# A two-layer diffusion backbone step: three temporaries for the pair products, a feed-forward in three parts, another pace for w_ada

## The chip, the cores and the metric

The kernel runs on one core of a Trainium2 chip. The metric is the device time of one execution in microseconds, as the median of several runs. The engines are TensorE (PE in the profile, its weight loads PEld), VectorE (DVE), ScalarE (ACT), GpSimd (POOL) and SyncE (SP), each with its own instruction queue that it works off in order. All DMAs go through the queues of SP and POOL but for three small ones at the start.

## The reference, cut to what matters

Each of two layers applies a token-mixing sub-layer and a SwiGLU feed-forward, both between normalisations, with scales, shifts and gates that come from a conditioning vector through `w_ada`. There are 128 context and 512 latent tokens, so 640 rows of 1024 features, all in float32.

```python
for l in range(DEPTH):                                   # 2
    mod = jax.nn.silu(c) @ w_ada[l] + b_ada[l]           # 6 vectors of 1024
    sh1, sc1, g1, sh2, sc2, g2 = jnp.split(mod, 6, axis=-1)
    h = rms_norm(x, g_pre[0]) * (1 + sc1) + sh1
    # ... combined projection, windowed attention, neighbourhood attention, Fourier mixing, merge
    x = x + g1 * rms_norm(y, g_post[0])
    h = rms_norm(x, g_pre[1]) * (1 + sc2) + sh2
    g, u = jnp.split(h @ w_ffn_in, 2, axis=-1)           # each 640 x 2816
    x = x + g2 * rms_norm((jax.nn.silu(g) * u) @ w_ffn_out, g_post[1])
```

The change lies in the feed-forward: `h @ w_ffn_in` is 640 x 1024 by 1024 x 5632, and `w_ffn_out` takes 2816 features back to 1024.

## The kernel before

**Precision.** TensorE takes each float32 operand as a high and a low part (`whi` and `wlo` for weights, made by ScalarE at L172 and VectorE at L173; `hT_hi` and `hT_lo` for activations), and every product is three matmuls.

**The feed-forward (`ffn`, L1510).** The 2816 features are 22 tiles of 128 columns. `FFN_PARTS` cuts them into parts. For the tiles of one part the kernel first makes gate ("fg") and up ("fu") projections, evacuates them to `aT` as a high and a low part (`evac`, L1530 to L1544), and then multiplies `aT` by the part's rows of `w_ffn_out` and adds the result to `y` (`xstat`, L1402, with `acc_y`, L1577; ScalarE copies in the first part, VectorE adds in the others). A unit of `w_ffn_out` is 256 rows by 512 columns and serves two tiles of a part, for one half of the output and all five token tiles: 30 matmuls of 512 columns. The last part runs through `xstat_tiles` (L1419) instead: the first half of the output runs unit by unit, the second half token tile by token tile, so that each tile's norm (`tail`, L1466) can start while later tiles are still being multiplied. The steps of a tail (residual, square, scale, transposes, split) are put off by the fixed delays in `DELAYS`, and the first projection of the next layer (`mix_open`, L901) needs the first three tiles' results.

**Pairs.** Apart from the first `FFN_SINGLE` = 2 tiles, gate and up projections are made for two column tiles at a time with seven products instead of eight (`pair`, L731): token halves, row halves and the two tiles make a 2 x 2 by 2 x 2 block product. Each product is 12 matmuls of 320 columns. Sums of activations ("S") are made on chip by `sums` (L676); sums of weights (`wsum`) are made in HBM by DMAs (`sum_jobs`, L399), copies on SP's queue (L412) and accumulating additions on POOL's queue (L415), 16 jobs for each part and each of gate and up. Between products the results pass through four temporaries (`m1`, `u2`, `m5`, `u3`) of 128 x 320, and two sets of four alternate; ScalarE writes at L750 and L758, VectorE at L754, L764, L768 and L773, POOL at L765. The temporaries lie in the buffer `mt3`.

**The order of the work.** Everything is written out by a planner with its own clock (`step`, L319): each group of matmuls adds its length at 2.4 columns per ns, and whatever has come due is emitted after it: deferred tasks, sum jobs (every `SUM_DT` microseconds of that clock, 2.9 for layer 0 from 20.0 on, 5.5 for layer 1 from the start of layer 0's feed-forward), and steps of the `w_ada` generator (every `ADA_DT` = 5.0 during pairs and output units). What is left of the sum jobs is flushed at the start of `ffn`; what is left of the `w_ada` steps is flushed by `ada_finish` (L552) before the last part's output units.

**The w_ada side work (`ada_round`, L465).** During the feed-forward the product with `w_ada` runs on VectorE (L498 and L500): eight loads of 512 KB a round on SP's queue, two operations of 128 x 1024 for each, then three steps of lag (`ADA_LAG`), then 16 small matmuls that add over the partitions (L512). Layer 0's feed-forward holds four rounds and layer 1's one. Three buffers of the side tile hold loads ahead.

**Weights.** `wraw` has four buffers of 512 KB; `whi` and `wlo` have three buffers, each of which holds one full unit or two half units of a pair. Two further buffers (`alt_slot`, L129) serve fixed units at the changes of stage, among them the last unit of the first output half and the first unit of the second half of the last part.

Of the kernel before, what the change touches and what calls it, by code (L numbers as in the profile page):

```python
# [10 lines left out]
F32 = mybir.dt.float32  # L11
F32R = mybir.dt.float32r
AF = mybir.ActivationFunctionType
OP = mybir.AluOpType
# [3 lines left out]
T = 640  # L18
# [14 lines left out]
FFN_SINGLE = 2  # L33
ADA_MIX = ([(0, 2), (0, 3), (0, 4)], [(1, 3), (1, 4)])
ADA_FFN = ([(0, 5), (1, 0), (1, 1), (1, 2)], [(1, 5)])
FFN_PARTS = (4, 6, 6, 6)
SUMS_AT = (0.1, 0.2, 2.0, 3.0, 4.0, 5.0, 9.0, 99.0)
SUM_START, SUM_DT, SUM_ROWS = 20.0, (2.9, 5.5), 256
TICK = 2.5
ADA_DT, ADA_LAG = 5.0, 3  # L40
T_TOK, T_KO, T_V = 2.7, 0.9, 2.9
ADA_D0 = 2.1
T_COL, T_OUT, T_GM = 8.0, 5.2, 2.0
# [50 lines left out]
class Weights:  # L94
# [34 lines left out]
    def alt_slot(key):  # L129
# [3 lines left out]
        if kind in ("wo", "fo"):  # L133
            k0 = 0 if kind == "wo" else DFF // 128 - FFN_PARTS[-1]
            k1 = 6 if kind == "wo" else DFF // 128 - 2
# [152 lines left out]
class Kernel:  # L288
# [85 lines left out]
    def pair_ranges():  # L374


        n0 = 0
        for p, nt in enumerate(FFN_PARTS):
            first = n0 if p else FFN_SINGLE
# [351 lines left out]
    def pair(self, key, evac):  # L731

        nc, W = self.nc, self.W
        m1, u2, m5, u3 = (self.tmp[:, 4 * self.tmp_set + i, :] for i in range(4))
        self.tmp_set ^= 1

        def product(i, ps, first, last):
            w, x = W.part(key, i), self.left[i]()
            for k in range(4):
                for j, (p, q) in enumerate(((0, 0), (0, 1), (1, 0))):  # L740
                    nc.tensor.matmul(ps, w[p][:, k, :], x[q][:, k, :], start=first and k == 0 and j == 0,  # L741
                                     stop=last and k == 3 and j == 2, skip_group_check=True)

        def end(i):
            W.part_done(key, i)
            self.step(12 * 320 * PE_COL)
        psum = lambda: self.psum("mm")[:, :320]
        p1 = psum()
        product(0, p1, True, False)
        nc.scalar.activation(m1, p1, AF.Copy)  # L750
        end(0)
        p2 = psum()
        product(1, p2, True, False)
        nc.vector.tensor_tensor(u2, p2, m1, op=OP.add)  # L754
        end(1)
        p3 = psum()
        product(2, p3, True, False)
        nc.scalar.activation(m5, p3, AF.Copy)  # L758
        end(2)
        product(3, p1, False, True)  # L760
        evac(0, p1, 0)
        end(3)
        product(4, p2, False, True)
        nc.vector.tensor_tensor(u3, p2, m1, op=OP.add)  # L764
        nc.gpsimd.tensor_tensor(m5, m5, u3, op=OP.subtract)  # L765
        end(4)
        product(5, p3, False, True)
        nc.vector.tensor_tensor(u2, p3, u2, op=OP.subtract)  # L768
        evac(1, u2, 0)
        end(5)  # L770
        p4 = psum()
        product(6, p4, True, True)
        nc.vector.tensor_tensor(m1, p4, u3, op=OP.add)  # L773
        evac(0, m1, 1)
        evac(1, m5, 1)
        end(6)
# [733 lines left out]
    def ffn(self, l):  # L1510
        nc = self.nc
# [3 lines left out]
        if l + 1 < L:  # L1515
            self.sums_due, self.sums_at, self.sums_dt = deque(self.sum_jobs(l + 1)), self.vt, SUM_DT[1]
        for p, nt in enumerate(FFN_PARTS):
            last = p == len(FFN_PARTS) - 1
            aT = [self.fp.tile([128, 4, T], F32R, name=f"aT{i}", tag=f"mt{i}", bufs=1) for i in range(3)]
            both = aT[2].rearrange("p (a b) t -> p a b t", a=2)  # L1520

            def split_of(j, aT=aT, both=both):

                return (aT[0][:, j, :], aT[1][:, j, :]) if j < 4 else (both[:, 0, j - 4, :], both[:, 1, j - 4, :])

            def lhs(j, t, split_of=split_of):
                return tuple(self.cut(w, t) for w in split_of(j))
            gate = {}

            def evac(kind, n, gate=gate, split_of=split_of, n0=n0):  # L1530
                def f(src, g):
                    c0, c1 = HALVES[g]
                    if n not in gate:
                        gate[n] = self.fp.tile([128, T], F32, name="sg", tag="sg", bufs=2)
                    t = gate[n][:, c0:c1]
                    if kind == "fg":
                        nc.scalar.activation(t, src, AF.Tanh, scale=0.5)
                        nc.vector.scalar_tensor_tensor(t, t, 1.0, src, op0=OP.add, op1=OP.mult)
                        return
                    nc.vector.tensor_tensor(t, t, src, op=OP.mult)  # L1540
                    hi, lo = (w[:, c0:c1] for w in split_of(n - n0))
                    nc.scalar.activation(hi, t, AF.Copy, scale=0.5)
                    nc.vector.scalar_tensor_tensor(lo, t, 0.5, hi.bitcast(F32), op0=OP.mult, op1=OP.subtract)
                return f  # L1544

            first = n0
            if p == 0:
                first = FFN_SINGLE
                seq = [(kind, n) for n in range(first) for kind in ("fg", "fu")]
                self.tmp = self.fp.tile([128, 8, 320], F32, name="tmp", tag="mt3", bufs=1)  # L1550
                self.tmp_set = 0
                for g in range(2):
                    self.run_tasks(GTOK[g])
                    if g:
                        self.sums(self.z, SUMS_AT)
                    for kind, n in seq[:3]:
                        self.proj((l, kind, n), g, evac(kind, n), 4, HALVES)
                self.W.alt.clear()
                for kind, n in seq[3:]:
                    self.proj2((l, kind, n), evac(kind, n), HALVES)  # L1560
                self.run_tasks(("sums",))
                rounds = ADA_FFN[l]
                self.run_tasks(range(5))
                side = self.fp.tile([128, 5, D], F32, name="ada_side", tag="x", bufs=1)
                self.W.side_open([side[:, i, :] for i in range(2, 5)], 8 * len(rounds))
                self.ada = self.ada_rounds(rounds, side[:, 0:2, :])
                self.ada_acc, self.ada_dt = 0.0, ADA_DT
# [170 lines left out]
```

## Time and profile before

| | us |
|---|---|
| median of three runs (2206.36 to 2209.75) | 2206.68 |
| the profiled execution, its own time | 2209.04 |
| span of the profile, first to last instruction | 2207.3 |
| PE busy | 2109.3 |
| VectorE busy | 1287.2 |
| ScalarE busy | 911.7 |
| GpSimd busy | 541.7 |

In the profile, a row of the waits reads: who waited, for whom, total microseconds, times, longest. A row of the timeline reads: start, length, engine, line, operation, output and inputs, shapes, count, and in brackets the engine's idle time before it with what ended it. A row of a stretch reads: its bounds and length, then busy time and number of instructions for PE, PEld, VectorE, ScalarE and POOL, and last the granted clock of TensorE, the busy share of the DMA engines and GB/s. A row of a group reads: line, engine, operation, names, shapes, count, then busy time, mean ns of one, and idle time before them.

### The profile page before, as it was taken

How to read it: one execution, taken by the hardware profiler on the slowest of the kernel's cores; microseconds unless marked ns; L12 is line 12 of the kernel's file. 1: busy time of each engine (PE TensorE's matmuls, PEld its weight loads, DVE VectorE, ACT ScalarE, POOL GpSimd, SP SyncE). 2: the span in 40 equal slices, each digit the busy share in tenths (PEclk: the TensorE clock that was granted, in tenths of full speed). 3: DMA queues.
4: the chain of work that ended last, by engine and by line, in shares of the span. 5: the costliest groups of instructions: out<-in, count | busy, mean ns of one | idle time of the engine just before them, and what ended most of it. 6: DMA issues, size and time to landing. Idle time of an engine off the chain costs nothing.

```text
span 2207.3 us, 36184 instructions
## 1 busy us (share of the span) xinstructions
PE 2109.3 (96%) x13876; PEld 1945.7 (88%) x13876; DVE 1287.2 (58%) x2397; ACT 911.7 (41%) x1944; POOL 541.7 (25%) x815
## 2 busy tenths in 40 slices
PE   6999999999889999999679999999999999999998
PEld 4999989998778998989659999999988799989896
DVE  3555555553238686778754656555533586747475
ACT  3644543432235442434235544444323444424252
POOL 3122245443234111111132111343411320101002
PEclk9999999999999999999889999999999999999999
DMA  7433467777994765888665343556545445434353
GB/s 269 127 81 76 117 163 176 171 180 210 280 236 130 205 188 165 227 226 219 202 182 158 94 92 91 140 130 137 140 137 175 147 148 153 135 105 148 92 153 134
DMA packets 387213, 349.70 MB, mean 158 GB/s; under 512 B 17632, under 2 KB 344320, under 8 KB 386784
## 3 DMA queue, kind: packets, MB, share of 16 engines
q1 hardware_dynamic: 345744, 293.51, 42.2%
q0 software_dynamic: 40864, 53.64, 15.4%
q8 instruction: 109, 1.79, 0.3%
q14 instruction: 64, 0.52, 0.1%
q10 hardware_dynamic: 432, 0.25, 0.0%
HBM read 335.50 MB, written 95.72 MB: 195 GB/s over the span
## 4 chain that ended last, share of the span: by engine, by line
PE 61%; DVE 4%; ACT 2%; issue 1%; POOL 1%; DVEq 0%; POOLq 0%; ACTq 0%
PE ps_mm L741 20%; PE ps_mm L647 7%; PE ps_mm L648 7%; PE ps_mm L649 7%; PE ps_mm L1397 5%; PE ps_mm L1398 5%; PE ps_mm L1399 5%; PE ps_o L849 1%; PE ps_t L836 1%; DVE ada_side L500 1%; PE ps_s L809 1%; PE ps_s L810 1%; DVE wlo L173 1%; DVE x L1474 1%; POOL hT_lo L628 0%
## 5 line engine op out<-in xcount | busy, mean ns | idle before, releaser
L173 DVE TENSOR_TENSOR wlo<-wraw,whi 128x512 fp32r<-128x512 f32 (+1 forms) x453 | 405.9, 902 | 366.3 <-ACT whi L172 360.7
L647 PE MATMUL ps_mm<-hT_hi,whi 128*128 128x256 f32 (+2 forms) x1552 | 490.4, 316 | 7.3 <-ACT whi L172 5.8
L649 PE MATMUL ps_mm<-hT_hi,wlo 128*128 128x256 f32 (+2 forms) x1552 | 482.9, 311 | 4.0 <-DVE wlo L173 4.0
L172 ACT ACTIVATE whi<-wraw 128x512 fp32r<-128x512 f32 (+1 forms) x453 | 354.6, 790 | 310.9 <-PE ps_mm L1399 118.8
L648 PE MATMUL ps_mm<-hT_lo,whi 128*128 128x256 f32 (+2 forms) x1552 | 481.7, 310 | 0.0
L647 PEld LDWEIGHTS ps_mm<-hT_hi,whi 128*128 128x128 f32 x1552 | 293.6, 189 | 17.2 <-ACT whi L172 7.9
L649 PEld LDWEIGHTS ps_mm<-hT_hi,wlo 128*128 128x128 f32 x1552 | 293.1, 189 | 6.3 <-DVE wlo L173 6.3
L648 PEld LDWEIGHTS ps_mm<-hT_lo,whi 128*128 128x128 f32 x1552 | 293.2, 189 | 0.4
L741 PE MATMUL ps_mm<-S,whi 128*128 128x320 f32 x960 | 213.2, 310 | 2.8 <-DVE tmp L754 2.8
L741 PE MATMUL ps_mm<-hT_hi,whi 128*128 128x320 f32 x640 | 198.0, 309 | 4.8 <-ACT tmp L750 4.8
L741 PE MATMUL ps_mm<-hT_hi,wlo 128*128 128x320 f32 x640 | 197.3, 308 | 0.0
L741 PE MATMUL ps_mm<-hT_lo,whi 128*128 128x320 f32 x640 | 197.3, 308 | 0.0
L765 POOL TENSOR_TENSOR tmp<-tmp 128x320 f32<-128x320 f32 x40 | 54.4, 1360 | 567.2 <-DVE tmp L764 508.4
L741 PEld LDWEIGHTS ps_mm<-S,whi 128*128 128x128 f32 x960 | 159.9, 188 | 5.6 <-DVE tmp L754 4.3
L415 POOL DMA_DIRECT2D wsum<-in_w_ffn_in x128 | 119.6, 1022 | 181.3 <-DMA wsum<-wsum 149.8
L1397 PE MATMUL ps_mm<-whi,aT 128*128 128x512 f32 x400 | 159.3, 398 | 0.0
L1398 PE MATMUL ps_mm<-wlo,aT 128*128 128x512 f32 x400 | 158.9, 397 | 0.0
L1399 PE MATMUL ps_mm<-whi,aT 128*128 128x512 f32 x400 | 158.7, 397 | 0.0
L741 PE MATMUL ps_mm<-S,wlo 128*128 128x320 f32 x480 | 148.1, 309 | 0.0
L741 PEld LDWEIGHTS ps_mm<-hT_hi,whi 128*128 128x128 f32 x640 | 120.1, 188 | 7.0 <-ACT tmp L750 6.4
L647 PE MATMUL ps_mm<-o,whi 128*128 128x256 f32 (+1 forms) x384 | 121.6, 317 | 0.0
L741 PEld LDWEIGHTS ps_mm<-hT_lo,whi 128*128 128x128 f32 x640 | 120.1, 188 | 0.3
(236 smaller groups left out, 3978.7 us busy)
## 6 DMA issues: line engine op xcount, KB each, us to landing
wraw<-in_w_in SPq DMA_DIRECT2D x92, 512.0 KB, 4.1
wraw<-wsum SPq DMA_DIRECT2D x160, 256.0 KB, 3.4
wsum<-in_w_ffn_in POOLq DMA_DIRECT2D x96, 384.0 KB, 6.5
wraw<-in_w_ffn_in SPq DMA_DIRECT2D x120, 256.0 KB, 3.3
wraw<-in_w_ada SPq DMA_DIRECT2D x56, 512.0 KB, 4.8
wraw<-in_w_ffn_out SPq DMA_DIRECT2D x44, 512.0 KB, 4.7
ada_side<-in_w_ada SPq DMA_DIRECT2D x40, 512.0 KB, 5.5
wsum<-in_w_ffn_in SPq DMA_DIRECT2D x48, 384.0 KB, 4.7
```

What stands on the lines that cost most here:

```text
L172: self.k.nc.scalar.activation(hi, src, AF.Copy)
L173: self.k.nc.vector.tensor_tensor(lo, src, hi.bitcast(F32), op=OP.subtract)
L415: return lambda: nc.gpsimd.dma_start(out[r], src[r], accum_op=OP.add)
L500: nc.vector.scalar_tensor_tensor(acc[:, s, :], u.raw, c, acc[:, s, :], op0=OP.mult, op1=OP.add)
L647: nc.tensor.matmul(ps, wh, xh[:, c0:c1], start=(k == 0), stop=False)
L648: nc.tensor.matmul(ps, wh, xl[:, c0:c1], start=False, stop=False)
L649: nc.tensor.matmul(ps, wl, xh[:, c0:c1], start=False, stop=(k == K - 1))
L741: nc.tensor.matmul(ps, w[p][:, k, :], x[q][:, k, :], start=first and k == 0 and j == 0, stop=last and k == 3 and j == 2, skip_group_check= ...
L765: nc.gpsimd.tensor_tensor(m5, m5, u3, op=OP.subtract)
L1397: nc.tensor.matmul(ps, xh, u.hi[:, i, :], start=st and i == 0, stop=False)
L1398: nc.tensor.matmul(ps, xh, u.lo[:, i, :], start=False, stop=False)
L1399: nc.tensor.matmul(ps, xl, u.hi[:, i, :], start=False, stop=sp and i == 1)
```

## The change

The parts become 6, 8 and 8 tiles. With two single tiles in the first part, the pairs per part and projection become 2, 4 and 4 (before: 1, 3, 3 and 3). `aT` takes four buffers instead of three, `mt0` to `mt3`: the high parts of tiles 0 to 3 and 4 to 7 in the first two, the low parts in the others. The temporaries leave `mt3` for three tiles of their own; `u3` is written over `m1`, and from one pair to the next `m1` and `u2` swap places, while `m5` keeps its tile. Sum jobs become 96 a layer, of 256 KB in the first part and 512 KB in the others (before: 128 jobs, 128 KB and 384 KB), and are emitted every 3.6 (layer 0) or 7.5 (layer 1). The `w_ada` steps are emitted every 4.2.

```diff
-FFN_PARTS = (4, 6, 6, 6)
+FFN_PARTS = (6, 8, 8)
 SUMS_AT = (0.1, 0.2, 2.0, 3.0, 4.0, 5.0, 9.0, 99.0)
-SUM_START, SUM_DT, SUM_ROWS = 20.0, (2.9, 5.5), 256
+SUM_START, SUM_DT, SUM_ROWS = 20.0, (3.6, 7.5), 256
 TICK = 2.5
-ADA_DT, ADA_LAG = 5.0, 3
+ADA_DT, ADA_LAG = 4.2, 3
...
     def pair(self, key, evac):
-        m1, u2, m5, u3 = (self.tmp[:, 4 * self.tmp_set + i, :] for i in range(4))
-        self.tmp_set ^= 1
+        self.tmp = self.tmp[1], self.tmp[0], self.tmp[2]
+        m1, u2, m5 = self.tmp
...
         product(4, p2, False, True)
-        nc.vector.tensor_tensor(u3, p2, m1, op=OP.add)
-        nc.gpsimd.tensor_tensor(m5, m5, u3, op=OP.subtract)
+        nc.vector.tensor_tensor(m1, p2, m1, op=OP.add)
+        nc.gpsimd.tensor_tensor(m5, m5, m1, op=OP.subtract)
...
         product(6, p4, True, True)
-        nc.vector.tensor_tensor(m1, p4, u3, op=OP.add)
+        nc.vector.tensor_tensor(m1, p4, m1, op=OP.add)
...
         for p, nt in enumerate(FFN_PARTS):
-            aT = [self.fp.tile([128, 4, T], F32R, name=f"aT{i}", tag=f"mt{i}", bufs=1) for i in range(3)]
-            both = aT[2].rearrange("p (a b) t -> p a b t", a=2)
-            def split_of(j, aT=aT, both=both):
-                return (aT[0][:, j, :], aT[1][:, j, :]) if j < 4 else (both[:, 0, j - 4, :], both[:, 1, j - 4, :])
+            aT = [self.fp.tile([128, 4, T], F32R, name=f"aT{i}", tag=f"mt{i}", bufs=1) for i in range(4)]
+            def split_of(j, aT=aT):
+                return tuple(aT[i + j // 4][:, j % 4, :] for i in (0, 2))
...
-                self.tmp = self.fp.tile([128, 8, 320], F32, name="tmp", tag="mt3", bufs=1)
-                self.tmp_set = 0
+                self.tmp = [self.fp.tile([128, 320], F32, name=f"tmp{i}") for i in range(3)]
```

## The prediction

> **What bounds the kernel now.** I read the page first, then TensorE's waits, then the timeline at each long wait, and last the sums over stretches.
>
> ```profile
> span 2207.3 us, 36184 instructions
> PE 2109.3 (96%) x13876; PEld 1945.7 (88%) x13876; DVE 1287.2 (58%) x2397; ACT 911.7 (41%) x1944; POOL 541.7 (25%) x815
> ...
> PE ps_t L512 <- DVE ada_side L500: 15.2, 1, 15.2
> PE ps_mm L647 <- ACT hT_hi L627: 14.6, 3, 10.8
> ...
> PE ps_t L599 <- DVE nt L587: 7.7, 4, 5.8
> PE ps_mm L647 <- ACT whi L172: 5.8, 6, 1.9
> PE ps_s L809 <- DVE sm L811: 5.5, 3, 3.2
> PE ps_t L599 <- ACT y L608: 5.2, 1, 5.2
> ```
>
> TensorE is busy 96% of the span, and the change alters none of its matmuls: both cuts of the 22 feed-forward tiles make 20 pairs a layer and 22 output units. The time can move only through the 98 us in which PE is idle, and through the slow stretch behind each long idle. Those waits sit at a few places, and the change touches most of them.
>
> **A. The w_ada step (ADA_DT 5.0 to 4.2).** The step loop counts planner time: a pair is 7 x 1.6 = 11.2, an output unit 30 x 512/2400 = 6.4. One round takes 19 calls: 16 VectorE operations, two empty calls, and the matmuls of L512 in the 19th; layer 0 has four rounds, 76 calls, the last VectorE operation in call 73. Now, up to `ada_finish`, there are 20 pairs and 4 + 6 + 6 units, 224 + 102.4 = 326.4, so 326.4/5.0 gives 65 calls. Call 65 falls at the very end, and 8 operations are left over: 9 in a row.
>
> ```profile
> 1083.74 10.85 DVE L500 SCALAR_TENSOR_TENSOR ada_side<-ada_side,ada_st 128x1024 f32<-128x1024 f32 x9
> ...
> 1093.54 2.19 PE L512 MATMUL ps_t<-ada_side,ones 128*32 128x256 f32 x16 [15.15 <-DVE ada_side L500]
> 1095.66 0.80 PE L1397 MATMUL ps_mm<-whi,aT 128*128 128x512 f32 x1
> ...
> 1099.64 0.39 PE L1397 MATMUL ps_mm<-whi,aT 128*128 128x512 f32 x1
> 1099.88 0.39 PE L1398 MATMUL ps_mm<-wlo,aT 128*128 128x512 f32 x1
> ...
> 816.52 1.07 PE L512 MATMUL ps_t<-ada_side,ones 128*32 128x256 f32 x16
> ```
>
> After, 20 pairs and 6 + 8 units come to 224 + 89.6 = 313.6, and 313.6/4.2 gives 74 calls. The last VectorE operation is due at 73 x 4.2 = 306.6, four products ahead of the pairs' end; calls 75 and 76, an empty one and the matmuls, are left. VectorE would have to run four products (some 7 us) late for PE to wait. The removed time is 15.15 us, plus what PE loses behind it: 16 matmuls in 2.19 us where an undisturbed round takes 1.07, and nine matmuls from 1095.66 to 1099.64, 3.98 us, where nine at the usual 0.23 (the rows at 1099.64 and 1099.88) take 2.1. Together 15.15 + 1.1 + 1.9 = 18.1 us.
>
> The Trainium skill ("TensorE: Matmul & The Clock Gate", Part 1) says that an idle window of about 3.4 us halves the array's clock, and that about 3.4 us of work restores it. Here the matmuls are 0.44 us apart instead of 0.23, and the slow stretch lasts from 1093.54 to 1099.64, 6 us, so the trace agrees in kind, for longer. By the page the restart would cost 1.7 us and the term 16.9.
>
> **B. The end of layer 0's feed-forward (last part 8 tiles instead of 6).** There each token tile of the second half gets 4 units instead of 3, 24 matmuls instead of 18, while its norm chain on VectorE stays.
>
> ```profile
> 605.85:672.72 66.87, 60.69 (x268) 48.85 (x266) 30.18 (x43) 25.84 (x53) 22.58 (x32) 0.95 0.82 222
> 1095.66:1160.38 64.72, 48.67 (x208) 39.24 (x205) 34.65 (x47) 22.49 (x49) 21.58 (x29) 0.87 0.63 183
> 1700.26:1759.54 59.28, 58.63 (x267) 47.61 (x265) 30.42 (x41) 25.94 (x53) 15.13 (x24) 1.00 0.48 160
> ...
> L1474 DVE SCALAR_TENSOR_TENSOR x<-y,ss,x 128x1024 f32<-128x1024 f32 x5 | 7.4, 1488 | 1.9 <-POOL ss L567 1.9
> L1595 DVE TENSOR_TENSOR y<-y,ps_mm 128x512 f32<-128x512 f32 x10 | 6.7, 683 | 10.9 <-PE ps_mm L1399 10.9
> L606 DVE TENSOR_SCALAR y<-ps_t,a,sh 128x128 f32<-128x128 f32 x12 | 4.1, 399 | 0.0
> L587 DVE TENSOR_SCALAR y<-x,ss 128x1024 f32<-128x1024 f32 x4 | 4.0, 1011 | 5.7 <-POOL ss L567 5.7
> ...
> L1599 DVE TENSOR_TENSOR y<-y,gm 128x512 f32<-128x512 f32 x5 | 3.5, 693 | 4.2 <-ACT junk L635 4.2
> L628 DVE TENSOR_TENSOR hT_lo<-y,hT_hi 128x512 fp32r<-128x512 f32 x3 | 2.1, 689 | 1.2 <-ACT hT_hi L627 1.1
> ```
>
> The first three rows are the output stretches of mix 0, feed-forward 0 and mix 1 (busy time of PE, PEld, DVE, ACT and POOL); mix 1 runs 4 units a tile in 59.28 us with nearly no idle. The others are VectorE's groups near the second stretch. Per tile it owes 7.4/5 + 6.7/5 + 4.1/3 + 4.0/4 + 3.5/5 + 2.1/3 = 6.6 us, and PE gives it 18 x 0.23 = 4.2 us; with 24 matmuls 5.6. The middle stretch holds 180 matmuls (41.9 us) and 24 transposes (about 3.1), so 19.7 us too many, 1.9 already in A: 17.8, 16.05 of it the waits of 5.2 and 10.85. The widened cover saves at least 4 x 1.4 = 5.6 us. At most it becomes like mix 1, 15 us. The deferred steps are due at fixed planner times, so tile 2's transposes, due 9.2 after its end, now come before the last two units (at 20.5 of 23.0, counted from tile 0's end), not after all of them (due 16.9, and the matmuls end at 17.9). One split of the next projection's weights moves later for want of a free buffer: 1.3 us less in the middle of the chain, and hidden by the first projection. I take 11. The output matmuls themselves, the last tile and the kernel's own end stay.
>
> **C. The half-sums (96 jobs a layer instead of 128, larger, further apart).** Bytes are the same: 32 jobs x 128 KB and 96 x 384 before, 32 x 256 and 64 x 512 after. Copies go through SP's queue among the weight loads, additions through POOL's. In layer 0 the last is due at 20 + 127 x 2.9 = 388 now and 20 + 95 x 3.6 = 362 after.
>
> ```profile
> 610.05 3.58 POOL L415 DMA_DIRECT2D wsum<-in_w_ffn_in  x4
> 639.79 0.88 POOL L415 DMA_DIRECT2D wsum<-in_w_ffn_in  x1 [26.16 <-DMA wsum<-wsum]
> ...
> 652.60 0.69 PE L599 MATMUL ps_t<-ident,nt 128*128 128x128 f32 x2 [5.83 <-DVE nt L587]
> ...
> 652.70 0.98 POOL L415 DMA_DIRECT2D wsum<-in_w_ffn_in  x1 [0.94 <-DMA wsum<-wsum]
> ```
>
> Additions due by 364 start at 610.05, so the last one after would start near 620, before POOL's norm steps are wanted (90 + 18 matmuls of 0.233 us after 605.85, about 631). Now POOL stands 26.16 us before a late copy with those steps queued behind; PE waits 5.83. Mix 0's stretch is 66.87 against mix 1's 59.28: 7.6 is the most to gain, 0 the least, if the 512 KB transfers land as late. I take 5.5. Elsewhere in mix 0 the denser sums (512/3.6 against 384/2.9 KB, +7%) press on SP's weight loads and on POOL's bias loads; the whole-run waits for whi (5.8) and for L811 (5.5) are their present price. I charge 2, from -4 to +6. In layer 1 the last job moves from 698.5 to 712.5 after the feed-forward's start, still some 50 ahead of the output projection: nothing.
>
> **D. VectorE in the pair stretches.**
>
> ```profile
> 761.34:838.72 77.38, 75.58 (x521) 74.27 (x520) 64.62 (x106) 36.92 (x74) 14.85 (x17) 1.00 0.69 192
> 880.54:958.78 78.24, 76.39 (x523) 74.55 (x522) 65.03 (x109) 36.32 (x73) 14.91 (x17) 1.00 0.83 229
> 1000.61:1078.39 77.78, 75.97 (x523) 74.39 (x521) 64.35 (x109) 36.21 (x73) 16.23 (x19) 1.00 0.87 230
> 2082.44:2156.29 73.85, 73.85 (x506) 73.84 (x504) 53.34 (x95) 36.33 (x73) 8.21 (x6) 1.00 0.48 143
> ...
> L500 DVE SCALAR_TENSOR_TENSOR ada_side<-ada_side,ada_st 128x1024 f32<-128x1024 f32 x70 | 91.0, 1315 | 0.0
> ...
> SPq L153 <- DVE ada_side L500: 22.0, 21, 5.7
> ```
>
> Six pairs take 73.85 us without w_ada work and 3.5, 4.4 and 3.9 more with it; 1.07 each is L512, so 8.6 us is PE held up by VectorE. Up to the last operation, pairs now hold 224/5.0 x 16/19 = 37.7 operations, after (224 - 7)/4.2 x 16/19 = 43.5: 5.8 more at 91.0/70 = 1.3 us, 7.5 us, less whatever slack takes. Three long stretches also recover one time less than four, about 2.5. From 0 to 10, I take 6. Each pair of calls also issues 512 KB on SP, behind which weight loads queue while it waits for L500 (last row); four raw buffers cover that. Twenty fewer additions at L1582 (0.69 us) save VectorE work only in stretches where PE has no wait: nothing.
>
> **E. Three temporaries.** They add waits: POOL's m5 - m1 before L773 overwrites m1, and L750 and L758 (ScalarE) behind the evacuations of the pair before.
>
> ```profile
> 2129.39 1.20 POOL L765 TENSOR_TENSOR tmp<-tmp 128x320 f32<-128x320 f32 x1 [11.39 <-DVE tmp L764]
> ...
> 2132.80 0.48 DVE L773 TENSOR_TENSOR tmp<-ps_mm,tmp 128x320 f32<-128x320 f32 x1
> ...
> 2134.76 0.49 DVE L1540 TENSOR_TENSOR sg<-sg,tmp 128x320 f32<-128x320 f32 x1
> ...
> 2137.55 0.43 ACT L758 ACTIVATE tmp<-ps_mm 128x320 f32<-128x320 f32 x1
> ```
>
> POOL is done 2.2 us before L773; m5's last reader 2.3 us before L758. If that cover went, ScalarE's splits and with them PE's weights would queue behind VectorE. Cost 0, and the fourth mt buffer and the new split of tiles cost nothing either: their readers are earlier matmuls on the same in-order PE.
>
> **Sum.** -18.1 - 11 - 5.5 + 2 + 6 = -26.6. The profiled execution took 2209.04 us around its span; that gives 2182.4. It lay 2.4 above the median, 2206.68, from which I predict 2180.
>
> **The rivals.**
> 1. The tail does not shrink beyond the work bound and POOL stays blocked: B 5.6, C 0, so -18.1 - 5.6 + 2 + 6 = -15.7, 2191. For it: the due times are fixed numbers, and VectorE still owes 6.6 us to 5.6. Against: mix 1's stretch.
> 2. The larger transfers hold SP and POOL in mix 0: C 0 and +8 there: 2206.7 - 18.1 - 11 + 8 + 6 = 2192. For: DMA share 0.82 at mix 0's end. Against: the same bytes.
> 3. Slower: the temporaries bind. With VectorE later by more than the 2.3 us of E, L758 stalls ScalarE in every pair; from there each further microsecond costs one in each of 40 pairs. One gives 2180 + 40 = 2220. Against: the stretches with w_ada lose only some 0.5 us a pair.
> 4. It doesn't do what it says: w_ada's last round still hangs over, A 0: 2198. Against: the nine operations match the count.
>
> **Chances.** Forecast 0.62 (own range 2169 to 2189), rival 1 0.16, rival 2 0.10, rival 3 0.07, rival 4 0.05. The range 2164 to 2202 holds all but rival 3 and the far ends: low with A 18, B 15, C 7.6, D 0 and a small gain in mix 0. A change under 0.2%, 4.4 us, cannot be told from none. Faster by more has 0.88 (all but rival 3 and mixtures of rivals 1, 2 and 4), within it 0.05, slower 0.07.
>
> **What would show it.** A: L512's last wait gone and no nine L500 in a row. B: the output stretch of feed-forward 0 near 66 us (58.9 of work) with under 8 us of waits. C: POOL not idle before L415 after 625, mix 0's stretch near 61. D: the pair stretches of eight about 104 us where 98.5 is the work, L741 the longest wait. E: L750, L758 and L773 with no new releaser. It is wrong if feed-forward 0 keeps a wait over 10 us, or if pairs without w_ada work, in layer 1, take over 12.5 us.

## The result and the profile after

The changed kernel takes 2187.59 us (median of four runs, 2183.41 to 2188.79), beside 2207.7 us (four runs) for the kernel before in the same comparison: a ratio of 0.9905, with a 95% interval from 0.9888 to 0.9922. It is faster by 20.1 us; the prediction had 26.6 and 2180, and its range holds the time. The parts of the sum came out quite differently from the way they were put, and that is what the rest is about.

The profiled execution of the changed kernel took 2188.79 us. Up to the start of `ffn` lines keep their numbers; in `evac` and the rest of `ffn` they are one or two lower (the gate's sum is L1537, the up product L1539, ScalarE's high part L1541, VectorE's low part L1542). First the span and the busy times on the page of the changed kernel, then TensorE's waits in it (who waited, for whom, total us, times, longest).

```profile
span 2187.0 us, 36116 instructions
PE 2109.1 (96%) x13876; PEld 1944.0 (89%) x13876; DVE 1272.2 (58%) x2377; ACT 910.0 (42%) x1944; POOL 510.8 (23%) x783
```

```profile
PE ps_mm L741 <- ACT tmp L750: 14.7, 9, 2.9
PE ps_mm L647 <- ACT whi L172: 10.1, 4, 3.7
PE ps_mm L741 <- DVE tmp L754: 8.1, 12, 0.8
...
PE ps_mm L647 <- ACT hT_hi L627: 4.1, 3, 1.9
...
PE ps_t L599 <- DVE nt L587: 3.0, 4, 0.9
PE ps_t L599 <- DVE y L587: 2.8, 2, 2.3
```

The four long waits of the kernel before are gone: 15.2 us for L500, 10.8 for `hT_hi`, 5.8 for `nt` and 5.2 for `y`. No single wait is longer than 3.7 us outside the kernel's start. In their place, at the top, stand waits that hardly showed before: the pair products of L741, for ScalarE's copy (L750) and for VectorE's sum (L754).

The stretches of the changed kernel, in the order output of mix 0 and output of the last part of layer 0 (first fence), then the three pair stretches of layer 0's feed-forward (second fence); columns as in the prediction's rows, busy time of PE, PEld, VectorE, ScalarE, POOL, granted clock, DMA share, GB/s:

```profile
601.83:661.35 59.52, 58.87 (x268) 47.59 (x266) 30.37 (x43) 25.84 (x53) 17.12 (x26) 1.00 0.61 189
...
1073.08:1134.84 61.76, 59.04 (x269) 47.35 (x265) 34.12 (x48) 26.01 (x52) 21.46 (x28) 1.00 0.67 213
```

```profile
697.35:753.05 55.70, 50.56 (x338) 49.25 (x337) 44.97 (x73) 25.15 (x51) 7.34 (x7) 1.00 0.77 224
794.97:908.08 113.11, 104.18 (x708) 101.24 (x707) 91.96 (x150) 49.08 (x100) 17.43 (x19) 0.98 0.67 189
963.85:1072.08 108.23, 103.15 (x692) 100.59 (x690) 91.86 (x151) 48.42 (x99) 18.21 (x20) 0.98 0.81 224
sum 277.04, PE 257.89 PEld 251.07 DVE 228.79 ACT 122.66 POOL 42.97; mean PE 85.96 PEld 83.69 DVE 76.26 ACT 40.89 POOL 14.32
```

The same sum for the four pair stretches of the kernel before, whose single rows the prediction shows but for the first:

```profile
sum 258.01, PE 252.54 PEld 247.82 DVE 213.40 ACT 122.27 POOL 50.01; mean PE 63.14 PEld 61.95 DVE 53.35 ACT 30.57 POOL 12.50
```

Both kernels do the same 20 pairs, 246.2 us of matmuls at 73.85 us for six, and three rounds of L512 inside. Before, some 8.5 us were lost there; now it is about 27.6. Laid end to end from the two traces, the time went like this (minus is gained):

| stretch | us |
|---|---|
| mix 0 up to its output units (they start at 601.83 instead of 605.85) | -4.0 |
| output units of mix 0 (66.87 to 59.52) | -7.4 |
| L512 at the end of layer 0's feed-forward: 15.15 of wait, and 16 matmuls that run at their usual speed | -16.2 |
| last output units of layer 0 (64.72 for 180 matmuls, now 61.76 for 240, which are 13.95 us more work) | -16.9 |
| pair stretches of layer 0 (258.0 to 277.0) | +19.0 |
| from there to the end: mix 1 +2.5, first projections of layer 1 +1.5, feed-forward 1 +1.3 | +5.3 |
| total | -20.2 |

### The profile page after: what moved, and what is told of

It is laid out like the page before. It is cut to its first block, busy times and chain, and to the rows that moved or that the text cites. A ratio compares the mean times of both kernels' runs of the same rounds, so it can differ in the third digit from the quotient of the medians.

```text
span 2187.0 us, 36116 instructions
## 1 busy us (share of the span) xinstructions
PE 2109.1 (96%) x13876; PEld 1944.0 (89%) x13876; DVE 1272.2 (58%) x2377; ACT 910.0 (42%) x1944; POOL 510.8 (23%) x783
## 4 chain that ended last, share of the span: by engine, by line
PE 55%; DVE 7%; ACT 3%; issue 3%; DMA 1%; POOL 1%; DVEq 0%; ACTq 0%; SPq 0%; POOLq 0%
PE ps_mm L741 15%; PE ps_mm L647 7%; PE ps_mm L648 6%; PE ps_mm L649 6%; PE ps_mm L1397 5%; PE ps_mm L1398 5%; PE ps_mm L1399 5%; PE ps_o L849 1%; DVE wlo L173 1%; DVE ada_side L500 1%; PE ps_t L836 1%; ACT whi L172 1%; DVE sg L1539 1%; PE ps_s L809 1%; PE ps_s L810 1%
## 5 line engine op out<-in xcount | busy, mean ns | idle before, releaser
L647 PEld LDWEIGHTS ps_mm<-hT_hi,whi 128*128 128x128 f32 x1552 | 294.3, 190 | 22.2 <-ACT whi L172 12.5
L649 PEld LDWEIGHTS ps_mm<-hT_hi,wlo 128*128 128x128 f32 x1552 | 293.9, 189 | 4.9 <-DVE wlo L173 4.9
L741 PE MATMUL ps_mm<-S,whi 128*128 128x320 f32 x960 | 214.1, 311 | 8.1 <-DVE tmp L754 8.1
L741 PE MATMUL ps_mm<-hT_hi,whi 128*128 128x320 f32 x640 | 199.8, 312 | 14.7 <-ACT tmp L750 14.7
L741 PE MATMUL ps_mm<-hT_hi,wlo 128*128 128x320 f32 x640 | 198.5, 310 | 0.0
L741 PE MATMUL ps_mm<-hT_lo,whi 128*128 128x320 f32 x640 | 198.4, 310 | 0.0
L765 POOL TENSOR_TENSOR tmp<-tmp,tmp 128x320 f32<-128x320 f32 x40 | 52.9, 1323 | 590.7 <-DVE tmp L764 482.9
L741 PEld LDWEIGHTS ps_mm<-S,whi 128*128 128x128 f32 x960 | 160.5, 189 | 11.3 <-DVE tmp L754 11.2
L741 PE MATMUL ps_mm<-S,wlo 128*128 128x320 f32 x480 | 148.3, 309 | 0.0
L741 PEld LDWEIGHTS ps_mm<-hT_hi,whi 128*128 128x128 f32 x640 | 120.9, 189 | 19.0 <-ACT tmp L750 17.3
L741 PEld LDWEIGHTS ps_mm<-hT_lo,whi 128*128 128x128 f32 x640 | 121.0, 189 | 0.1
L741 PEld LDWEIGHTS ps_mm<-hT_hi,wlo 128*128 128x128 f32 x640 | 121.1, 189 | 0.0
L1333 ACT ACTIVATE sg<-ps_mm 128x384 f32<-128x384 f32 x96 | 41.7, 435 | 190.3 <-PE ps_mm L649 190.2
```

Of the source, the lines that this page charges most:

```text
L647: nc.tensor.matmul(ps, wh, xh[:, c0:c1], start=(k == 0), stop=False)
L649: nc.tensor.matmul(ps, wl, xh[:, c0:c1], start=False, stop=(k == K - 1))
L765: nc.gpsimd.tensor_tensor(m5, m5, m1, op=OP.subtract)
L1333: lambda ps, g: self.nc.scalar.activation(sg[:, GROUPS[g][0]:GROUPS[g][1]], ps, AF.Tanh, scale=0.5))
```

## The experiments

The theory after reading the two traces: the changed kernel gains some 41 us by A, B and C as meant, and loses 19 us in the pair stretches of layer 0 because more `w_ada` operations fall there. Rivals: the loss comes from the three temporaries, from the longer parts, or from the larger transfers of the sums. Each ratio is to the kernel before, run on the same chip; the medians come from several chips, on which the kernel before took 2207.5 to 2209.1 us, so kernels are better compared by their ratios. "Held" below is the time of the pair stretches of layer 0 beyond their 246.2 us of matmuls and beyond L512 (and, where a wait for the last round follows, up to the last pair matmul); "operations" are the `w_ada` operations of VectorE (L498 and L500, 64 in all) that start inside these stretches.

| kernel | median us | ratio, interval | held us | operations |
|---|---|---|---|---|
| before | 2207.7 | 1 | 8.4 | 36 |
| before, three temporaries | 2206.87 | 0.9993 [0.9984, 1.0003] | 10.0 | 36 |
| before, `ADA_DT` 4.2 | 2207.38 | 1.0002 [0.9992, 1.0012] | 24.7 | 44 |
| changed | 2187.59 | 0.9905 [0.9888, 0.9922] | 27.6 | 46 |
| changed, `ADA_DT` 5.0 | 2198.9 | 0.9963 [0.995, 0.9976] | 18.4 | 39 |
| changed, parts 8, 8, 6 | 2200.14 | 0.9957 [0.9943, 0.9972] | 25.7 | 47 |
| changed, later start of w_ada | 2180.62 | 0.9876 [0.9855, 0.9897] | 22.2 | 44 |
| changed, uneven pace | 2171.98 | 0.9836 [0.982, 0.9853] | 16.7 | 35 |
| changed, very uneven pace | 2167.36 | 0.9806 [0.9784, 0.9828] | 9.2 | 29 |
| changed, most w_ada operations left out | 2167.61 | 0.9811 [0.9792, 0.983] | 7.2 | 14 of 16 |
| changed, later split | 2176.15 | 0.985 [0.9834, 0.9867] | 16.2 | 46 |
| changed, very uneven pace and later split | 2157.7 | 0.9768 [0.9754, 0.9783] | 2.4 | 29 |

**The pace alone, on the kernel before.**

```diff
-ADA_DT, ADA_LAG = 5.0, 3
+ADA_DT, ADA_LAG = 4.2, 3
```

> The kernel before with ADA_DT 4.2 alone. Theory: 326.4/4.2 = 77 calls, nothing hangs over, so the wait of 15.2 us and its slow restart go (-18); the pair stretches of feed-forward 0 hold 44 instead of 37 operations, +9; the end of the feed-forward keeps its two waits of 5 and 11 us; together about -9, near 2198. Rival (pace costs nothing in the pairs): -18, near 2189.

It gave 2207.38 us, no difference at all, beside 2198 expected and 2189 for the rival. TensorE's waits in this kernel:

```profile
PE ps_mm L741 <- ACT tmp L750: 16.2, 11, 2.4
PE ps_mm L647 <- ACT hT_hi L627: 14.3, 3, 10.6
...
PE ps_t L599 <- DVE nt L587: 7.5, 4, 5.6
...
PE ps_t L599 <- ACT y L608: 5.2, 1, 5.2
```

The wait of L512 for L500 is gone, and L750's takes its place. Eight operations moved from the tail into the pair stretches, and held time rose from 8.4 to 24.7 us: 16.3, where the expectation had 9. What A removes, 18 us, is paid back there nearly in full.

**The old pace, on the changed kernel.**

```diff
-ADA_DT, ADA_LAG = 4.2, 3
+ADA_DT, ADA_LAG = 5.0, 3
```

> The changed kernel with ADA_DT back at 5.0, all else as changed. The planner then makes 313.6/5.0 = 62 calls before the last part, so 11 VectorE operations are left over instead of none. Theory (the closer pace buys the end of the overhang with VectorE work inside the pair stretches): one wait of L512 on L500 of some 19 us plus 3 us of slow restart comes back; the pair stretches of feed-forward 0 hold 38 operations instead of 46 and lose about 10 us of their excess (277 to about 267); together about +12, near 2199. Rival (the excess comes from longer runs of pairs or from fewer temporaries, not from the pace): the pair stretches stay at 277 and the time is near 2209.

2198.9 us, as expected. The wait at the end of the feed-forward is back, longer than in the kernel before, and a part of the time held in the pairs is gone (27.6 to 18.4 us):

```profile
PE ps_t L512 <- DVE ada_side L500: 22.5, 1, 22.5
PE ps_mm L741 <- ACT tmp L750: 12.1, 8, 2.5
```

So inside the changed kernel the pace is worth some 11 us, more than on the kernel before: with 20 pairs but only 14 units ahead of the last part, the old pace leaves more over. But held time does not go back to the 8.4 us of the kernel before, though only three more operations fall in the pairs. Of the 18.4 us, 7.0 are lost in the first stretch (56.18 us for 49.2 of matmuls), where VectorE waits 3.8 us for the load of its first `w_ada` operation. So the closer pace alone does not make the loss.

**The three temporaries alone, on the kernel before.**

```diff
-        m1, u2, m5, u3 = (self.tmp[:, 4 * self.tmp_set + i, :] for i in range(4))
-        self.tmp_set ^= 1
+        self.tmp = self.tmp[1], self.tmp[0], self.tmp[2]
+        m1, u2, m5 = self.tmp
...
-        nc.vector.tensor_tensor(u3, p2, m1, op=OP.add)
-        nc.gpsimd.tensor_tensor(m5, m5, u3, op=OP.subtract)
+        nc.vector.tensor_tensor(m1, p2, m1, op=OP.add)
+        nc.gpsimd.tensor_tensor(m5, m5, m1, op=OP.subtract)
...
-        nc.vector.tensor_tensor(m1, p4, u3, op=OP.add)
+        nc.vector.tensor_tensor(m1, p4, m1, op=OP.add)
...
-                self.tmp = self.fp.tile([128, 8, 320], F32, name="tmp", tag="mt3", bufs=1)
-                self.tmp_set = 0
+                self.tmp = [self.fp.tile([128, 320], F32, name=f"tmp{i}", tag=f"tm{i}", bufs=1) for i in range(3)]
```

> The kernel before with the three rotating temporaries alone, as separate tiles; parts, sums and pace as before. Theory: no new wait binds (POOL is done over 1.2 us before L773 and the last reader of m5 over 0.8 us before L758), so 0 within 2 us, near 2207, pair stretches 24.6, 77.4, 78.2, 77.8 and 73.8 without w_ada work. Rival (the temporaries bind where VectorE is late): the three stretches with w_ada work grow by 3 us or more each, over 2215.

2206.87 us, the interval holds 1. This rival falls: rotating three tiles instead of two sets of four costs nothing that can be seen. Their use is another one; they leave the room in which the fourth `mt` buffer and with it parts of eight tiles fit.

**The parts in another order.**

```diff
-FFN_PARTS = (6, 8, 8)
+FFN_PARTS = (8, 8, 6)
```

> The changed kernel with the parts in the order 8, 8, 6: the last part has 3 units a token tile again, everything else as changed. Theory (the end of feed-forward 0 shrank because each tile's norm chain on VectorE, 6.6 us, got 5.6 us of matmuls instead of 4.2): the waits on y L608 and hT_hi L627 come back, 10 to 16 us, the last output stretch is again near 64 us for 180 matmuls, and the time near 2202. Rival (the end shrank because nothing hung over from w_ada, so the tail began undisturbed): the waits stay under 4 us, near 2188.

2200.14 us. With the short part last, both long waits at the end of layer 0 are back to a tenth of a microsecond:

```profile
PE ps_mm L741 <- ACT tmp L750: 18.2, 12, 2.5
PE ps_mm L647 <- ACT hT_hi L627: 14.5, 3, 10.8
...
PE ps_t L599 <- ACT y L608: 5.2, 1, 5.2
```

The last stretch takes 62.9 us for 180 matmuls, beside 61.8 for 240. It is the eight tiles in the last part, hence 24 matmuls between one token tile's norm and the next, that remove B's waits. They are worth 15.1 us in the stretch, counted for equal work, and 12.5 in the whole time.

**The pace of the half-sums, both ways.** Whether the last copies land before mix 0's output units hangs on when the last interval ends. The interval alone was lengthened on the changed kernel, and shortened on the kernel before:

```diff
-SUM_START, SUM_DT, SUM_ROWS = 20.0, (3.6, 7.5), 256
+SUM_START, SUM_DT, SUM_ROWS = 20.0, (3.87, 7.5), 256
```

> The changed kernel with layer 0's sum jobs every 3.87 instead of 3.6, so that the last is due at 387.7 as in the kernel before. Theory (POOL's wait for late sum copies held the norm steps of mix 0's output stretch): that stretch goes back from 59.5 to 63 to 67 us, with a wait of PE on nt L587 of some 6 us; near 2193. Rival (something else shortened it): it stays under 60, near 2187.

```diff
-SUM_START, SUM_DT, SUM_ROWS = 20.0, (2.9, 5.5), 256
+SUM_START, SUM_DT, SUM_ROWS = 20.0, (2.69, 5.5), 256
```

> The kernel before with layer 0's sum jobs every 2.69 instead of 2.9, so that the last of the 128 is due at 361.6, as after the change. Theory: mix 0's output stretch goes from 66.9 to about 60 us, and the denser sums cost or gain up to 4 us ahead of it; near 2200. Rival: only fewer and larger transfers help, the stretch stays near 67, near 2207.

The changed kernel with sums as late as before took 2198.27 us (0.9958 [0.994, 0.9975]), its output stretch of mix 0 67.65 us instead of 59.52; the kernel before with earlier sums 2203.33 us (0.9979 [0.997, 0.9989]), with 59.51 us instead of 66.87. TensorE's wait for the norm in the first of the two:

```profile
PE ps_t L599 <- DVE nt L587: 8.6, 3, 7.1
```

In the stretch both agree with C to within a microsecond, 7.4 to 8.1 us. In the whole time they don't: 4.1 us on the one side, 10.7 on the other (the expectations had 7 and 6), and the six runs of the first spread from 2192.37 to 2203.31. The profiled one is the fastest of these, so where its slower runs lose the rest stays open.

**Without most of the w_ada operations.** This kernel leaves out terms 1 to 6 of the eight of each `w_ada` product in both feed-forwards (48 of the 64 operations in layer 0); loads and steps stay.

```diff
                 if k == 0:
                     nc.vector.tensor_scalar(acc[:, s, :], u.raw, c, None, op0=OP.mult)
-                else:
+                elif k == 7:
                     nc.vector.scalar_tensor_tensor(acc[:, s, :], u.raw, c, acc[:, s, :], op0=OP.mult, op1=OP.add)
```

> The changed kernel without six of the eight terms of each w_ada product on VectorE during the feed-forwards (terms 1 to 6 are left out, so the scales and gates made there are not the reference's); loads, calls and matmuls stay. Theory: with 4 instead of 16 operations a round, VectorE is no longer full and all pair stretches come to their work, 49.2 and 98.5 us plus 1.1 for each L512: about 250 instead of 277 in feed-forward 0 and 5 us less in feed-forward 1, near 2157. Rival (temporaries, long runs, or the DMAs of the side loads): the excess of some 27 us stays, near 2185.

2167.61 us (2160.87 to 2170.66, the profiled run being the fastest), some 10 above what was expected, and held time falls from 27.6 to 7.2. The three temporaries, the longer parts and the larger transfers of the sums are all still there, so the loss in the pair stretches is mostly the work itself on VectorE. The loads are still there too, and they keep a part of it: 3.2 of the 7.2 us are lost in the first stretch, where VectorE still waits 3.8 us for the first load.

**Moving the w_ada work into output units.** The planner counts a unit of the output stretches more than its length, so that the steps fall there; the interval is lengthened to keep their number.

```diff
-ADA_DT, ADA_LAG = 4.2, 3
+ADA_DT, ADA_LAG = 6.4, 3
...
                 W.done(u)
+                self.ada_acc += 1.9 * dur
                 self.step(dur)
```

> The changed kernel, with the w_ada calls spread unevenly: every 6.4 of planner time during pairs, and three times as fast during output units (each unit counts 2.9-fold), still 75 calls before the last part. Theory (VectorE is full in the pair stretches and has room in the output stretches): about 30 instead of 46 operations in the pairs of feed-forward 0, up to 16 x 1.2 = 19 us less, pairs near 258 instead of 277, output stretches still 41.9 and 55.8; near 2170. Rival (long runs or temporaries): pairs stay near 277 and the time near 2187. A second rival: the bunched operations delay the evacuations and the splits of the output stretches, which grow by 5 to 10 us.

2171.98 us: 24 accumulations now run in output units (10 and 14), which take as long as before, and held time is 16.7 instead of 27.6 us. The gain in the pairs, 11 us, is less than the 19 expected, in the main because the first stretch kept its 55.6 us. Why shows in the waits of ScalarE and VectorE in the first pair stretch of the changed kernel (with the uneven pace the load comes 3.7 us late, much the same):

```profile
ACT aT L1541 <- DVE sg L1539: 15.2, 7, 3.8
...
DVE ada_side L498 <- DMA ada_side<-in_w_ada: 4.2, 1, 4.2
```

VectorE stands at the first `w_ada` operation for 4.2 us because its load has not landed, and the evacuations of the pairs are queued behind it. Two more kernels put that right, the first by a later start (with an interval of 4.1, so that the steps still end in time) and the second together with a stronger shift into the output units:

```diff
-ADA_DT, ADA_LAG = 4.2, 3
+ADA_DT, ADA_LAG = 4.1, 3
...
-                self.ada_acc, self.ada_dt = 0.0, ADA_DT
+                self.ada_acc, self.ada_dt = -8.0, ADA_DT
```

> The changed kernel with the first w_ada step of the layer-0 feed-forward put off by about 8 us of counted work (count starts at -8.0, interval 4.1 instead of 4.2 so that the steps still end before the last output part). If 4 us of the first pair stretch go to VectorE standing 4.25 us at a w_ada operation whose load has not landed (theory), that stretch falls from 55.7 to about 51.5 us, the first VectorE operation of w_ada no longer waits above 1.5 us for its load, and the time is 2183 to 2184. Rival: the load is as late behind a later step, or the operations put off crowd the second and third stretch by as much: 2186 to 2189.

```diff
-ADA_DT, ADA_LAG = 4.2, 3
+ADA_DT, ADA_LAG = 9.0, 3
...
                 W.done(u)
+                self.ada_acc += 4.06 * dur
                 self.step(dur)
...
-                self.ada_acc, self.ada_dt = 0.0, ADA_DT
+                self.ada_acc, self.ada_dt = -8.0, ADA_DT
```

> The changed kernel with the w_ada steps paced even more unevenly: a unit of the output stretches counts 5.06-fold, the interval is 9.0 and the count starts at -8.0, so that the first step comes later and most VectorE work of w_ada falls in output stretches. If the loss in the pair stretches of layer 0 is VectorE's w_ada work there (theory), they take 250 to 256 us together (277.0 in the changed kernel, 264.1 with a weight of 2.9 and an interval of 6.4) and the time is 2160 to 2167 us. Rival: the output stretches, which held 24 accumulations without growing, now grow (43.0 and 57.2 so far), because evacuations of the output units queue behind them or the steps wait for their loads; the sum of pair and output stretches then stays and the time is 2170 to 2178.

The later start alone took 2180.62 us. Its first stretch is 50.81 us instead of 55.70, without a wait for the load, the other two stay (112.3 and 108.6); layer 1, whose round had a wait of 2.8 us of the same kind, gains 3.4 us in its first stretch, which the expectation had not counted. The very uneven pace took 2167.36 us. Its pair stretches:

```profile
694.77:745.79 51.02, 49.98 (x339) 49.25 (x337) 39.97 (x71) 25.55 (x51) 11.52 (x14) 1.00 0.79 222
788.82:889.78 100.96, 99.55 (x673) 98.50 (x672) 84.69 (x140) 49.56 (x100) 13.88 (x13) 1.00 0.74 203
950.73:1054.26 103.53, 99.99 (x675) 98.48 (x673) 86.09 (x145) 48.58 (x99) 16.04 (x15) 1.00 0.82 221
sum 255.51, PE 249.53 PEld 246.23 DVE 210.75 ACT 123.69 POOL 41.44; mean PE 83.18 PEld 82.08 DVE 70.25 ACT 41.23 POOL 13.81
```

255.5 us without any L512 inside, 9.2 held, as the theory put it. The output stretches that now hold 35 of the 64 operations grew by some 3 us alone, one wait of L512 (2.1 us) and about 1 us of slower matmuls behind it, so the rival falls. The time lies just above the expectation's upper end of 2167.

**How VectorE's lateness reaches TensorE.** In the second pair stretch of the changed kernel, VectorE is busy 91.96 of 113.11 us, so it has a fifth of the time free, and yet TensorE loses 12.6 us. Three engines at one such place: ScalarE, VectorE and TensorE of the changed kernel (start, length, engine, line; in brackets the idle time before, and what ended it).

```profile
822.35 0.47 ACT L1541 ACTIVATE aT<-sg 128x320 fp32r<-128x320 f32 x1 [3.98 <-DVE sg L1539]
...
825.04 0.47 ACT L1541 ACTIVATE aT<-sg 128x320 fp32r<-128x320 f32 x1 [1.69 <-DVE sg L1539]
826.47 0.47 ACT L1541 ACTIVATE aT<-sg 128x320 fp32r<-128x320 f32 x1 [0.96 <-DVE sg L1539]
826.85 0.61 ACT L172 ACTIVATE whi<-wraw 128x512 fp32r<-128x512 f32 x1
827.37 0.42 ACT L750 ACTIVATE tmp<-ps_mm 128x320 f32<-128x320 f32 x1
```

```profile
819.49 1.90 DVE L500 SCALAR_TENSOR_TENSOR ada_side<-ada_side,ada_st 128x1024 f32<-128x1024 f32 x1
821.32 0.48 DVE L768 TENSOR_TENSOR tmp<-ps_mm,tmp 128x320 f32<-128x320 f32 x1
821.83 0.49 DVE L1539 TENSOR_TENSOR sg<-sg,tmp 128x320 f32<-128x320 f32 x1
```

```profile
825.82 0.31 PE L741 MATMUL ps_mm<-S,wlo 128*128 128x320 f32 x1
827.84 0.42 PE L741 MATMUL ps_mm<-hT_hi,whi 128*128 128x320 f32 x1 [1.71 <-ACT tmp L750]
```

An accumulation of 1.90 us stands ahead of the end of an up tile on VectorE. ScalarE waits for that (L1541, three times, 6.6 us), and behind it in its own queue stand a split of weights and the copy of the next pair's first product (L750), for which it has all it needs. TensorE's fourth product, which adds to the same PSUM tile, waits for the copy. So ScalarE's queue hands the delay on. If that is right, the order alone can take it away: the split of the second half of an up tile is written behind the next pair's first copy.

```diff
                     hi, lo = (w[:, c0:c1] for w in split_of(n - n0))
-                    nc.scalar.activation(hi, t, AF.Copy, scale=0.5)
-                    nc.vector.scalar_tensor_tensor(lo, t, 0.5, hi.bitcast(F32), op0=OP.mult, op1=OP.subtract)
+                    def split():
+                        nc.scalar.activation(hi, t, AF.Copy, scale=0.5)
+                        nc.vector.scalar_tensor_tensor(lo, t, 0.5, hi.bitcast(F32), op0=OP.mult, op1=OP.subtract)
+                    if g and self.hold:
+                        self.late.append(split)
+                    else:
+                        split()
...
         nc.scalar.activation(m1, p1, AF.Copy)
+        self.flush_late()
         end(0)
...
```

Here `hold` is set while pairs are written, and `flush_late` writes out what `late` holds; it is called again after the last pair of a part.

> The changed kernel with one order altered: in the pair units, the split of the second half of an up tile (ScalarE's copy of its high part, which waits for VectorE's product, and VectorE's low part) is written behind the next pair's copy of its first product, not ahead of it; no operation is added or left out. The changed kernel's pair stretches of layer 0 take 277.0 us with 13.2 us of TensorE waits for that copy. If ScalarE standing at the split hands VectorE's lateness on to TensorE (theory), those waits fall to below 5 us, the pair stretches to 265 to 270 us and the time to 2176 to 2181. Rival: VectorE's work itself is the limit and ScalarE's place in the chain is incidental; the waits move to VectorE's sums in the pair (8.1 us in the whole of the changed kernel), the pair stretches stay above 274 us and the time at 2185 to 2189.

> The later split together with the most uneven pacing tried (units of the output stretches counted 5.06-fold, interval 9.0, count from -8.0), which took 2167.4 us with pair stretches of 255.5 us and 3.3 us of waits for the copy. Where the pacing has left VectorE its slack, little is left for the later split: if both cure one cause (theory), 2164 to 2168 with pair stretches of 252 to 255; if they cure two (rival), as much more as the later split brings by itself, 2155 to 2160.

The later split alone took 2176.15 us, with pair stretches of 265.7 us instead of 277.0:

```profile
sum 265.68, PE 253.78 PEld 248.00 DVE 226.54 ACT 122.01 POOL 42.95; mean PE 84.59 PEld 82.67 DVE 75.51 ACT 40.67 POOL 14.31
```

Lines of this kernel's `pair` are five or six higher: L746 is the matmul, L755 and L760 are what L750 and L754 were. TensorE's waits in it, over the whole run:

```profile
PE ps_mm L746 <- DVE tmp L760: 10.7, 13, 1.3
...
PE ps_mm L746 <- ACT tmp L755: 4.5, 3, 2.2
```

The waits for the copy fall from 14.7 to 4.5 us in the whole run (none is left in the second pair stretch), those for VectorE's sum rise only from 8.1 to 10.7. All 46 operations are still in the pairs; 11.3 us of the 27.6 held there were lost to the order. (How much of the 8.4 us of the kernel before would come back by it was not tried.) The theory holds and its rival, that the waits would move to VectorE's sums, falls.

Both together took 2157.7 us, 30 us less than the changed kernel. Its pair stretches:

```profile
693.20:743.25 50.05, 49.72 (x339) 49.25 (x338) 40.03 (x71) 25.91 (x51) 11.63 (x14) 1.00 0.80 227
786.27:885.10 98.83, 98.74 (x673) 98.47 (x672) 84.49 (x140) 49.99 (x100) 13.85 (x13) 1.00 0.76 207
946.04:1045.79 99.75, 99.02 (x676) 98.47 (x674) 85.42 (x145) 48.96 (x99) 16.03 (x15) 1.00 0.84 230
sum 248.63, PE 247.48 PEld 246.19 DVE 209.94 ACT 124.86 POOL 41.51; mean PE 82.49 PEld 82.06 DVE 69.98 ACT 41.62 POOL 13.84
```

Held time is 2.4 us, less than in any other kernel, the one without most of the operations among them. Here the expectation that both edits cure one cause was wrong: the later split took another 6.9 us from pair stretches in which only 2.9 us of waits for the copy were left, and 9.7 us from the median (8.4 by the ratios). Of the 6.9 us, 4.8 are idle time of TensorE (255.51 less 249.53, now 248.63 less 247.48). Waits for the copy make up 2.6 of them and waits for VectorE's sum 2.3: those fall from 2.9 to 0.3 and from 3.0 to 0.7 us. The other 2.1 are busy time of TensorE. So the waits that the profile names are not the whole of such a loss: in the second stretch of the changed kernel they are 7.1 and 1.8 us out of 12.6, and TensorE's own busy time is larger, 104.2 us for the work of 98.5 and two rounds of L512, at a granted clock of 0.98.

## Why the prediction was right and where it was wrong

**A** was right as far as it went: L512's wait is gone, its 16 matmuls take 1.0 us, and the last output units start at full speed (granted clock 1.00 in that stretch, 0.87 before). 15.15 + 1.1 + 1.9 = 18.1 came off that place. But on the kernel before it is no net gain: the pace alone changed nothing (1.0002 [0.9992, 1.0012], with 16.3 us more held in the pairs). The prediction charged the moved operations under D, and there it charged too little.

**B** was mis-sized to the safe side. The term taken was 11 of a range from 5.6 to 15; the stretch went from 19.7 us too many to 2.8 (61.76 less 240 matmuls, 55.8, and 3.1 of transposes), of which 1.9 is A's: 15.0, the upper bound. The argument for the bound, that the stretch becomes like mix 1's, was the better one. That the eight tiles do it is shown by the reversed parts, where both waits and 15.1 us of the stretch come back. The first rival, a tail that keeps its waits, falls.

**C** was right in place and mechanism. POOL, which stood 26 us before a late copy, now issues its last addition before the norm steps are wanted:

```profile
605.83 0.87 POOL L415 DMA_DIRECT2D wsum<-in_w_ffn_in  x1
608.99 0.87 POOL L415 DMA_DIRECT2D wsum<-in_w_ffn_in  x1 [2.29 <-DMA wsum<-wsum]
628.61 0.97 POOL L637 TENSOR_SCALAR ss<-ss 128x1 f32<-128x1 f32 x2 [18.74 <-ACT junk L635]
```

7.4 us came off, against 5.5 taken and 7.6 as the most. The charge of 2 us for denser sums elsewhere in mix 0 is not borne out: the output units start 4.0 us earlier. But this number has little weight. In the seven experiments on the changed kernel that leave mix 0 as it is they start anywhere between 596.8 and 603.3 us, and in the three profiles of the kernel before with its own sums between 601.0 and 605.9. The second rival, that larger transfers hold mix 0 up, falls all the same.

**D** is the step that failed. The prediction put "5.8 more" operations at 1.3 us, less slack, and "From 0 to 10, I take 6". Held time rose by 19. Two things were wrong. First, the count: it took the share of calls that carry work, 16 of 19, as even, but the empty calls of a round come together, at its end. Where they fall decides. In the pairs there are 46 operations instead of 36, ten more and not six; L500 in the second and third pair stretch, by its starts, is

```profile
L500 DVE SCALAR_TENSOR_TENSOR ada_side<-ada_side,ada_st x14: 1276/1279/1902, 809.0 to 877.3; 128x1024 f32<-128x1024 f32 x14
...
L500 DVE SCALAR_TENSOR_TENSOR ada_side<-ada_side,ada_st x17: 1276/1279/1897, 965.9 to 1067.6; 128x1024 f32<-128x1024 f32 x17
```

where the kernel before had nine in each of three. At 1.3 us these are 13 us. Second, the price: the prediction treated VectorE's work as the bound, so that slack could only make it cheaper. It costs more than its own length. The 19 us are of two kinds.

The first stretch, which lost nothing before, loses 6.5 (55.70 us for 49.2 of matmuls). VectorE stands 4.2 us before the first load there, and with the later start the stretch was 4.9 us shorter. The trace of before has that wait too, but smaller and without a loss for TensorE:

```profile
DVE ada_side L498 <- DMA ada_side<-in_w_ada: 1.4, 1, 1.4
```

The long stretches lose 12.6 us more than before. Counted by pair, in the kernels that keep all operations and the order of the split:

| kernel | operations a pair | held us a pair |
|---|---|---|
| changed, very uneven pace | 1.63 | 0.47 |
| changed, uneven pace | 1.81 | 0.65 |
| before | 1.83 | 0.48 |
| changed, `ADA_DT` 5.0 | 1.94 | 0.72 |
| before, `ADA_DT` 4.2 | 2.22 | 1.09 |
| changed, later start | 2.25 | 1.30 |
| changed | 2.31 | 1.33 |

How close the operations stand sets most of the loss, and more than in proportion. At the same density the changed kernel loses some 0.2 us a pair more, 3 us in all; no run separates the cause of that. Nor does any run show the 2.5 us that the prediction took off for one recovery less.

The way by which it reaches TensorE could have been read in the trace of before: ScalarE, in order, holds the next pair's copy behind a split that waits for VectorE (the later split got 11.3 us back). The row for L1542 and L1540 of the kernel before, ScalarE's waits in its third pair stretch, was there:

```profile
ACT aT L1542 <- DVE sg L1540: 16.3, 9, 3.4
ACT sg L1537 <- DVE tmp L768: 7.0, 3, 3.0
```

In the changed kernel's second stretch the same wait is nearly twice as long:

```profile
ACT aT L1541 <- DVE sg L1539: 30.5, 13, 4.0
```

**E** was right: nothing on the kernel before, and no new releaser at L750, L758 or L773: in the changed kernel these wait for TensorE alone. The third rival, binding temporaries, falls; so does the fourth, since no operation hangs over.

That the total came out near is luck, because errors of both signs met: A as put, B 4 and C 2 us better, mix 0 some 6 better than charged, D 13 worse, and some 5 us lost after layer 0 that no step had. No experiment was spent on these; the later start brought 3.4 us in layer 1's first stretch.

What would have shown the prediction wrong did not come: no wait over 10 us is left in layer 0's feed-forward, and pairs without `w_ada` work take 98.45 / 8 = 12.3 us. What it named for D, "about 104 us" for eight pairs, was 113.1 and 108.2, and L741's wait is the longest, as it said. For B it named a stretch near 66 us and for C one near 61; they were 61.8 and 59.5.

## What to carry to other kernels

Work that is moved out of a wait at the end of a stage has to be counted, operation by operation, where it lands; if it lands in a stage where the same engine already holds others up, the wait is paid there, as on the kernel before, where the pace alone gained 18 us and lost them again. Ask first which stage has room (the output units took 35 operations and grew by 3 us) and move the work there. And look at what stands behind a waiting instruction on a third engine: writing one split a few instructions later brought 11 us without taking any work away.

## What the runs showed that was not expected

Here the busy share of an engine said little about whether it held others up. In the second pair stretch VectorE is busy for 91.96 of 113.11 us (81%) in the changed kernel, and TensorE loses 12.6 us; in the best kernel it is busy for 84.49 of 98.83 us (85%), and TensorE loses 0.4.

The other is the scatter of a stage that nothing was changed in. Up to mix 0's output units the changed kernel and seven of its variants issue the same instructions, and still arrive there between 596.8 and 603.3 us; the output stretch itself, 59.5 us, repeats to a few hundredths. A difference of a few microseconds in mix 0 between two profiles is therefore no evidence for an edit, and that holds for the 4.0 us in the table of stretches above.
